# Low parts of the second weights on VectorE in two of three chunks, row sums pinned, stores behind the writes

## The chip, the cores and the metric

The kernel runs on one core of a Trainium2 chip. The metric is device time in microseconds, as the median of several executions. TensorE does the matmuls, VectorE (DVE) and GpSimd (POOL) the element-wise work on buffers in SBUF, ScalarE (ACT) activations and copies, and SyncE (SP) issues most of the DMA.

## What is computed

One encoder layer over 2304 rows (2048 of a prompt and 256 of a sample) of 1024 features, in float32. The mixing groups come first and are not touched by the change. Behind them stands the feed-forward part, then a final RMSNorm:

```python
x = x + group_output_norm(y_attn, y_four, y_mem, g_grp) @ w_out
hf = rmsnorm(x, g_ffn) @ w_ff1
x = x + jnp.square(jax.nn.relu(hf)) @ w_ff2
...
return rmsnorm(x, g_final)
```

## The kernel before

**The feed-forward part**, from about 865 us of the span to its end, handles the rows in NCH = 3 chunks (c = 0, 1, 2) of 768 rows: two halves of three blocks (NT = 3) of 128 rows. Both products are made by a scheme of Strassen's type: matrices are cut in 2 x 2 blocks, and seven products (i = 1 to 7) of sums of blocks replace eight. Each operand is a float32 number in two parts, a high part in TensorE's reduced format and the remainder as a low part, and each product is made of three matmuls: high by high, low by high, high by low. `hi_of` (L103) makes a high part on ACT, `lo_of` (L106) subtracts it from the source on VectorE, or on POOL if told so.

**The loop** (L1306 to L1340) goes over steps n. Step n makes one product of the first matmul (`product`, L1072: 12 matmuls of 128x384, into PSUM tiles pa, pb, pc, pd) and one half of a product of the second (`half_step`, L1167: 9 matmuls of 128x512, into y), 14 steps (LAG) behind. The halves of the last group of the last chunk run alone at the end, since no first products are left (`last_half_step`, which fills y and yl). Each half step needs one tile of the second weights w_ff2: `split2` (L1050) makes its high part w2h and low part w2l, each with two buffers; before the change w2l is made by POOL in all 336 half steps. `splitA` makes the high and low parts ah and al of the activations (POOL makes sums ms and m of them at L987). The loads of weights and of rows go through `granule` (L891) on SP's queue.

**The end of a chunk.** VectorE adds the products y into accumulators acc (L323, L326), and POOL and VectorE add accumulators to each other. `finish` (L1238) returns functions that the loop pops one for each step (`pending`, L1337): three calls of `write` (L1226) for each half of the rows. `measure` has ACT take sums of squares (tile fk, L1224), `write` has POOL make the reciprocal root (tile ff, L137 and L138), VectorE scale both halves of a row block (L1235), and then issues two stores to out_dram, that of the left half (n = 0) on ACT's queue and that of the right half on SP's. The next chunk's accumulators use the buffers of the ones written, and are loaded from X2d on SP's queue (`load_acc`).

**Row sums.** `late_rows` (L1283) is called three times in the middle of chunk 1, at n = 152, 160 and 168. Each call loads four tiles xl of the last chunk's normalized rows from XnT, lets POOL make four differences (`row_sums`, L819), and stores them to Xn, from where chunk 2 reads its operands XT.

**The order.** The program is written by a framework that runs a timeline estimate (`schedule_with_timeline_sim=True`, L1379) and sets each engine's order by it: an instruction that is ready early by that estimate can be moved ahead of where it is written. On the chip each engine then goes in that fixed order. Before the change, the first two groups of row sums stand in the change from chunk 0 to chunk 1, some 40 steps ahead of where they are written.

Of the kernel before, what the change touches and what calls it, by code (L numbers as in the profile page):

```python
# [20 lines left out]
P = 128  # L21
# [13 lines left out]
CH = 768  # L35
NCH = T // CH
CT = CH // P
NT = CT // 2
# [55 lines left out]
def trunk(ctx, tc, x, mem, w_in, w_mem, w_out, w1, w2, gains, g_final, sinks, ident_d, dist_d, cdft_d, seq_d, y):  # L94
    nc = tc.nc
    pe, act, dve, pool, sp = nc.tensor, nc.scalar, nc.vector, nc.gpsimd, nc.sync
# [5 lines left out]
    def hi_of(out, src, scale=1.0):  # L102
        act.activation(out, src, AF.Copy, scale=scale)  # L103

    def lo_of(out, src, hi, eng=None):
        (eng or dve).tensor_tensor(out=out, in0=src, in1=hi.bitcast(F32), op=ALU.subtract)  # L106
# [29 lines left out]
    def rstd_of_means(st):  # L136
        pool.tensor_scalar(out=st[:, 0:1], in0=st[:, 0:1], scalar1=st[:, 1:2], scalar2=EPS, op0=ALU.add, op1=ALU.add)  # L137
        pool.tensor_tensor(out=st[:, 0:1], in0=st[:, 0:1], in1=mhalf[:, 0:1], op=ALU.pow)  # L138
# [7 lines left out]
    if True:  # L146
# [100 lines left out]
        def stage(i, name):  # L247
            if i % 2:
                return stage4k(name)
            return apool.tile([P, D], F32, tag="Qs", bufs=2, name=name)  # L250
# [48 lines left out]
        for mp in (3, 2, 0, 1, 4):  # L299
            for kh in range(2):  # L300
                s = stage(kh, f"wins_{mp}_{kh}")
                sv = s.rearrange("p (k n) -> p k n", k=4)
                sp.dma_start(sv, w_in[kh * 512:(kh + 1) * 512, mp * 256:(mp + 1) * 256].rearrange("(k p) n -> p k n", p=P))
                for j in range(4):
                    k = kh * 4 + j
# [16 lines left out]
        def add(o, a, b):  # L322
            TT(out=o, in0=a, in1=b, op=ALU.add)  # L323
# [260 lines left out]
        for i, name in enumerate(order):  # L584
            g = int(name[1:])
# [17 lines left out]
    if True:  # L603
# [156 lines left out]
        def c_mem(pair, h, mh, ml):  # L760
            b0 = pair[0]["b"]
            vm = memkv[pair[0]["r"]][1]
            if h % 2 == 0:
                pair[0]["mo"] = ps_o.tile([P, 2, 256], F32, tag="o", name=f"otm_{b0}_{h}")
            po = pair[0]["mo"]
            for j in range(2):
                w = vm[:, j, h].rearrange("p l d -> p (l d)")
                mm(po[:, h % 2], w, mh[:, j], j == 0, False)
                mm(po[:, h % 2], w, ml[:, j], False, j == 1)
            if h % 2 == 1:  # L770
                pair[0].setdefault("ot", []).append(evac_o(po.rearrange("p a (b t) -> p (a b) t", b=2), f"otms_{b0}_{h}"))
            if h < 3:
                return None
            ots = pair[0]["ot"]

            def fin():
                for i, B in enumerate(pair):
                    ytile(B)
                    recip(B, NH, NMH)
                    combine(B, NH, [ots[g // 2][:, (g % 2) * 2 + i] for g in range(4)], f"om_{B['b']}")  # L780
                    normalise(B, 768, 256, 25)
            return fin
# [34 lines left out]
        def row_sums(b11, b21, b12, b22):  # L817
            for o, u, v, i in ((b11, b12, b11, 5), (b12, b22, b12, 7), (b22, b22, b11, 6), (b21, b22, b21, 4)):
                pool.tensor_tensor(out=o, in0=u, in1=v, op=ALU.subtract)  # L819
                yield i, o  # L820
# [70 lines left out]
        def granule(name, src, second=False):  # L891
            if second:
                t = rp.tile([P, 512], F32, tag="w2r", bufs=5, name=name)
            else:
                t = lp.tile([P, 512], F32, tag="w1r", bufs=9, name=name)
            if src is not None:
                sp.dma_start(t, src)
            return t
# [27 lines left out]
        n = 0  # L926
        while n < len(units) + LB or later:
            if n < len(units):
                kind, b0, i, h = units[n]
# [6 lines left out]
            if 0 <= m < len(units):  # L936
                kind, b0, i, h = units[m]
# [5 lines left out]
            if 0 <= m < len(units):  # L943
                kind, b0, i, h = units[m]
# [8 lines left out]
                if kind == "m":  # L953
                    f = c_mem(pairs[b0], h, *pend_b.pop(m))
# [17 lines left out]
    if True:  # L972
# [13 lines left out]
        def ptt(o, a, b, op):  # L986
            pool.tensor_tensor(out=o, in0=a, in1=b, op=op)  # L987
# [62 lines left out]
        def split2(r):  # L1050
            if 0 <= r < len(steps2):
                k = steps2[r]
                nm = "_".join(map(str, k))
                s = src2.pop(k)
                h = rp.tile([P, 512], F32R, tag="w2h", bufs=2, name=f"w2h_{nm}")
                l = rp.tile([P, 512], F32R, tag="w2l", bufs=2, name=f"w2l_{nm}")
                hi_of(h, s)
                lo_of(l, s, h, pool)
                ops2[k] = (h, l)


# [74 lines left out]
        acc, ybank = {}, {}  # L1136
# [19 lines left out]
        def last_group(c, g):  # L1156
            return c == NCH - 1 and g == NG - 1
# [57 lines left out]
        def gains_of(c):  # L1215
            return [granule(f"gf{n}_{c}", g_final[n * 512:(n + 1) * 512].partition_broadcast(P)) for n in range(2)]
# [3 lines left out]
        def measure(c, b, n, t):  # L1220
            if (c, b) not in stats:
                stats[c, b] = late[0].tile([P, 2], F32, tag="fst", bufs=6, name=f"ff_{c}_{b}")
            jk = late[0].tile([P, 512], BF16, tag="fjk", bufs=1, name=f"fk{n}_{c}_{b}")
            act.activation(jk, t, AF.Square, scale=D ** -0.5, accum_out=stats[c, b][:, n:n + 1])  # L1224

        def write(c, b, hv, gf, end=False):  # L1226
            r0 = c * CH + b * P
            st = stats.pop((c, b))
            rstd_of_means(st)
            for n in range(2):  # L1230
                o = hv[n]
                if end and n == 0:
                    act.activation(o, o, AF.Copy, scale=st[:, 0:1])
                else:
                    dve.scalar_tensor_tensor(out=o, in0=o, scalar=st[:, 0:1], in1=gf[n], op0=ALU.mult, op1=ALU.mult)  # L1235
                (sp if n else act).dma_start(y[r0:r0 + P, n * 512:(n + 1) * 512], o)

        def finish(c, g, i):  # L1238


            A = lambda i, t: acc[c, i, t]
            last = c == NCH - 1
            if i == 1 and g == NG - 1:
                acc[c, "g"] = gains_of(c)
            if last_group(c, g):
                for t in range(NT):
                    if i == 2:
                        measure(c, t, 0, A(2, t))
                        ptt(A(2, t), A(2, t), acc[c, "g"][0], ALU.mult)
                    elif i == 7:  # L1250
                        measure(c, NT + t, 1, A("x", t))
                    elif i == 4:
                        measure(c, NT + t, 0, A(4, t))
            else:
                for t in range(NT):
                    if i == 1:
                        acc[c, "x", t] = granule(f"x22_{c}_{t}", X2d[c * CT + NT + t][:, 512:1024])
                    elif i == 2:
                        ptt(A(2, t), A(2, t), A(1, t), ALU.add)
                    elif i == 5:  # L1260
                        ptt(A("x", t), A("x", t), A(5, t), ALU.add)
                    elif i == 6:
                        ptt(A(6, t), A(6, t), A(1, t), ALU.add)
                    elif i == 7:
                        add(A(7, t), A(7, t), A(6, t))
                        ptt(A(6, t), A(6, t), A(5, t), ALU.add)
                        add(A("x", t), A("x", t), A(7, t))
                    elif i == 4:
                        add(A(4, t), A(4, t), A(7, t))
                    elif i == 3:  # L1270
                        add(A(3, t), A(3, t), A(6, t))
                    if not last:
                        for o, h, k in ((2, 0, 2), (7, 1, "x"), (4, 1, 4), (3, 0, 3)):
                            if i == o:
                                measure(c, h * NT + t, 1 if k in ("x", 3) else 0, A(k, t))
            if g == NG - 1 and i == 4:
                return [lambda t=t: write(c, NT + t, [A(4, t), A("x", t)], acc[c, "g"]) for t in range(NT)]
            if g == NG - 1 and i == 3 and not last:
                return [lambda t=t: write(c, t, [A(2, t), A(3, t)], acc[c, "g"]) for t in range(NT)]
            return []  # L1280


        def late_rows(t):  # L1283
            a, b = (XnT[(NCH - 1) * CT + o + t].rearrange("p (n t) -> p n t", n=2) for o in (0, NT))
            g = [granule(f"xl{i}_{t}", s) for i, s in enumerate((a[:, 0], a[:, 1], b[:, 0], b[:, 1]))]
            for i, o in row_sums(*g):
                sp.dma_start(Xn[NCH - 1, i][:, :, t * P:(t + 1) * P], o.rearrange("p (k t) -> p k t", k=KH))

# [17 lines left out]
        for n in range(len(steps1) + LAG):  # L1306
# [17 lines left out]
            load_acc(r + 3)  # L1324
            operand1(n + 2)
            split2(r + 2)
            splitA(r + 2)
            sumA(r + 4)
            if n < len(steps1):
                product(n)  # L1330
                c, j, i = steps1[n]
                if j == NJ - 1 and c + 1 < NCH:
                    load_x(c + 1, i)
            if r >= 0:
                c, g, i, e = steps2[r]
# [48 lines left out]
```

## Time and profile before

| | |
|---|---|
| median of 3 runs | 2340.67 us (2337.38 to 2342.37) |
| the profiled execution | 2344.84 us |
| its span | 2343.0 us |
| TensorE busy | 2229.2 us, 95% |
| VectorE busy | 1561.4 us, 67% |
| POOL busy | 1139.7 us, 49% |
| ACT busy | 1003.4 us, 43% |

Durations are those of the profiled execution. Busy time of TensorE can hold slow matmuls: the granted clock, as a share of 2.4 GHz, tells how fast they ran. A row of a timeline gives the start in the span, the duration, the engine, the line, the operation, result and operands, the count, and in brackets the idle time before it and the instruction that ended it. Counts in brackets in a table of stretches are instructions.

### The profile page before, as it was taken

How to read it: one execution, taken by the hardware profiler on the slowest of the kernel's cores; microseconds unless marked ns; L12 is line 12 of the kernel's file. 1: busy time of each engine (PE TensorE's matmuls, PEld its weight loads, DVE VectorE, ACT ScalarE, POOL GpSimd, SP SyncE). 2: the span in 40 equal slices, each digit the busy share in tenths (PEclk: the TensorE clock that was granted, in tenths of full speed). 3: DMA queues.
4: the chain of work that ended last, by engine and by line, in shares of the span. 5: the costliest groups of instructions: out<-in, count | busy, mean ns of one | idle time of the engine just before them, and what ended most of it. 6: DMA issues, size and time to landing. Idle time of an engine off the chain costs nothing.

```text
span 2343.0 us, 35879 instructions
## 1 busy us (share of the span) xinstructions
PE 2229.2 (95%) x12464; PEld 2005.2 (86%) x12464; DVE 1561.4 (67%) x2781; ACT 1003.4 (43%) x2353; POOL 1139.7 (49%) x1023
## 2 busy tenths in 40 slices
PE   7999996999999999999999899999999999999996
PEld 6999995887788878999999788999998889999984
DVE  7333476777677767888888986555557765555567
ACT  6333356766566654444444433222224342222224
POOL 3554031113123035777777685444444765444476
PEclk9999998999999999999999999999999999999998
DMA  8886347445444368766666887555557675555543
GB/s 298 309 296 246 100 136 280 138 148 158 149 145 156 132 238 298 252 222 228 222 229 222 311 262 272 192 191 190 190 191 268 196 258 187 190 189 190 190 163 99
DMA packets 207116, 488.05 MB, mean 208 GB/s; under 512 B 19799, under 2 KB 63319, under 8 KB 204631
## 3 DMA queue, kind: packets, MB, share of 16 engines
q1 hardware_dynamic: 192896, 446.86, 56.2%
q0 software_dynamic: 6848, 29.24, 3.6%
q10 hardware_dynamic: 7191, 9.65, 1.2%
q8 instruction: 99, 1.62, 0.3%
q14 instruction: 82, 0.67, 0.1%
HBM read 341.76 MB, written 144.83 MB: 208 GB/s over the span
## 4 chain that ended last, share of the span: by engine, by line
PE 67%; DVE 8%; DMA 4%; ACT 2%; issue 2%; POOL 1%; SPq 0%; POOLq 0%; ACTq 0%; DVEq 0%
PE y L100 26%; PE op L100 8%; PE pc L100 8%; PE pb L100 8%; PE pa L100 8%; PE pd L100 4%; DMA X2d<-xr 1%; DVE acc L323 1%; PE s L100 1%; PE ot L100 1%; PE t L687 1%; DVE p L661 1%; DMA XTl<-Xn 1%; DVE al L106 1%; PE otm L100 1%
## 5 line engine op out<-in xcount | busy, mean ns | idle before, releaser
L106 POOL TENSOR_TENSOR w2l<-w,w2h 128x512 fp32r<-128x512 f32 x336 | 484.3, 1443 | 494.8 <-ACT w2h L103 490.2
L100 PE MATMUL y<-w2l,ah 128*128 128x512 f32 x966 | 380.9, 395 | 6.4 <-POOL w2l L106 6.4
L100 PE MATMUL y<-w2h,al 128*128 128x512 f32 x966 | 381.9, 396 | 0.0
L100 PE MATMUL y<-w2h,ah 128*128 128x512 f32 x966 | 360.7, 398 | 17.6 <-DVE acc L323 9.0
L103 ACT ACTIVATE ah<-m 128x384 fp32r<-128x384 f32 x240 | 125.8, 524 | 509.5 <-PE y L100 488.0
L106 DVE TENSOR_TENSOR al<-m,ah 128x384 fp32r<-128x384 f32 x240 | 182.9, 763 | 180.2 <-ACT ah L103 167.6
L323 DVE TENSOR_TENSOR acc<-acc,y 128x512 f32<-128x512 f32 x378 | 244.3, 680 | 24.1 <-PE y L100 20.0
L100 PEld LDWEIGHTS y<-w2h,ah 128*128 128x128 f32 x966 | 183.3, 190 | 45.2 <-DVE acc L323 12.1
L100 PE MATMUL pc<-XTh,w1s 128*128 128x384 f32 x768 | 218.8, 340 | 0.8 <-DVE m L323 0.3
L100 PE MATMUL pa<-XTh,w1s 128*128 128x384 f32 x768 | 215.7, 337 | 0.7 <-ACT w1s L103 0.5
L100 PE MATMUL pb<-XTh,w1s 128*128 128x384 f32 x768 | 214.5, 336 | 0.7 <-ACT m L1095 0.7
L103 ACT ACTIVATE w2h<-w 128x512 fp32r<-128x512 f32 x336 | 207.3, 617 | 10.9 <-DMA w1s<-W1D 4.5
L100 PEld LDWEIGHTS y<-w2h,al 128*128 128x128 f32 x966 | 183.3, 190 | 33.1
L100 PEld LDWEIGHTS y<-w2l,ah 128*128 128x128 f32 x966 | 183.3, 190 | 30.4 <-POOL w2l L106 7.8
L100 PE MATMUL pj<-hl_x,winh 128*128 128x256 f32 x720 | 206.1, 288 | 0.7 <-DVE hl_x L106 0.7
L100 PE MATMUL pj<-hh_x,winh 128*128 128x256 f32 x720 | 203.5, 288 | 1.3 <-ACT hh_x L103 1.3
L100 PE MATMUL pj<-hh_x,winl 128*128 128x256 f32 x720 | 204.5, 286 | 0.0
L1068 DVE SCALAR_TENSOR_TENSOR m<-m 128x384 f32<-128x384 f32 x192 | 159.0, 828 | 42.5 <-ACT m L1095 39.0
L100 PEld LDWEIGHTS pc<-XTh,w1s 128*128 128x128 f32 x768 | 142.9, 190 | 10.4 <-DVE m L323 1.4
L100 PEld LDWEIGHTS pb<-XTh,w1s 128*128 128x128 f32 x768 | 141.2, 188 | 8.9 <-ACT m L1095 1.0
L100 PEld LDWEIGHTS pa<-XTh,w1s 128*128 128x128 f32 x768 | 141.6, 188 | 8.3 <-ACT w1s L103 0.8
L100 PEld LDWEIGHTS pj<-hl_x,winh 128*128 128x128 f32 x720 | 139.3, 194 | 1.3 <-DVE hl_x L106 1.2
(243 smaller groups left out, 5181.4 us busy)
## 6 DMA issues: line engine op xcount, KB each, us to landing
w1s<-W1D SPq DMA_DIRECT2D x224, 512.0 KB, 3.5
W1D<-w1s SPq DMA_DIRECT2D x112, 512.0 KB, 3.6
w<-in_w_dram SPq DMA_DIRECT2D x208, 256.0 KB, 3.8
w<-W2T SPq DMA_DIRECT2D x192, 256.0 KB, 3.6
w2r<-in_w_dram SPq DMA_DIRECT2D x16, 1024.0 KB, 7.3
W2T<-w2r POOLq DMA_DIRECT2D x16, 1024.0 KB, 6.2
XTl<-Xn SPq DMA_DIRECT2D x21, 768.0 KB, 7.7
qb<-Qd SPq DMA_DIRECT2D x18, 768.0 KB, 6.3
```

Of the source, the lines that this page charges most:

```text
L100: pe.matmul(out, lhsT, rhs, start=start, stop=stop, skip_group_check=more)
L103: act.activation(out, src, AF.Copy, scale=scale)
L106: (eng or dve).tensor_tensor(out=out, in0=src, in1=hi.bitcast(F32), op=ALU.subtract)
L323: TT(out=o, in0=a, in1=b, op=ALU.add)
L661: dve.tensor_tensor_reduce(out=p[:, 0:n], in0=s[:, 0:n], in1=bias[:, u, c0:c0 + n], scale=1.0, scalar=nsink[:, u:u + 1], op0=ALU.add, op1= ...
L687: pe.transpose(t[:, j], p[:, j * P:(j + 1) * P], ident)
L1068: dve.scalar_tensor_tensor(out=r, in0=r, scalar=0.0, in1=r, op0=ALU.max, op1=ALU.mult)
```

## The change

It has three parts. The low part w2l is made by VectorE where the half step belongs to chunk 1 or 2 (k[0] is the chunk), 224 of 336; chunk 0's stay on POOL. The loads of `late_rows` are issued inside `tc.keep_in_program_order`, so that the scheduler leaves them where they are written. `finish` returns, through `rows`, first the three functions that write and then three that `store`: both halves of a row block go out by SP's queue, in functions popped three steps after the writes; only the very last rows (`end`) are stored by `write` as before.

```diff
--- before.py
+++ after.py
@@ -1055,7 +1055,7 @@
                 h = rp.tile([P, 512], F32R, tag="w2h", bufs=2, name=f"w2h_{nm}")
                 l = rp.tile([P, 512], F32R, tag="w2l", bufs=2, name=f"w2l_{nm}")
                 hi_of(h, s)
-                lo_of(l, s, h, pool)
+                lo_of(l, s, h, pool if k[0] == 0 else dve)
                 ops2[k] = (h, l)
 
 
@@ -1233,7 +1233,13 @@
                     act.activation(o, o, AF.Copy, scale=st[:, 0:1])
                 else:
                     dve.scalar_tensor_tensor(out=o, in0=o, scalar=st[:, 0:1], in1=gf[n], op0=ALU.mult, op1=ALU.mult)
-                (sp if n else act).dma_start(y[r0:r0 + P, n * 512:(n + 1) * 512], o)
+                if end:
+                    (sp if n else act).dma_start(y[r0:r0 + P, n * 512:(n + 1) * 512], o)
+
+        def store(c, b, hv):
+            r0 = c * CH + b * P
+            for n in range(2):
+                sp.dma_start(y[r0:r0 + P, n * 512:(n + 1) * 512], hv[n])
 
         def finish(c, g, i):
 
@@ -1274,15 +1280,22 @@
                             if i == o:
                                 measure(c, h * NT + t, 1 if k in ("x", 3) else 0, A(k, t))
             if g == NG - 1 and i == 4:
-                return [lambda t=t: write(c, NT + t, [A(4, t), A("x", t)], acc[c, "g"]) for t in range(NT)]
+                return rows(c, NT, 4, "x")
             if g == NG - 1 and i == 3 and not last:
-                return [lambda t=t: write(c, t, [A(2, t), A(3, t)], acc[c, "g"]) for t in range(NT)]
+                return rows(c, 0, 2, 3)
             return []
+
+        def rows(c, b0, i0, i1):
+            hv = [[acc[c, i0, t], acc[c, i1, t]] for t in range(NT)]
+            return ([lambda t=t: write(c, b0 + t, hv[t], acc[c, "g"]) for t in range(NT)] +
+                    [lambda t=t: store(c, b0 + t, hv[t]) for t in range(NT)])
 
 
         def late_rows(t):
             a, b = (XnT[(NCH - 1) * CT + o + t].rearrange("p (n t) -> p n t", n=2) for o in (0, NT))
-            g = [granule(f"xl{i}_{t}", s) for i, s in enumerate((a[:, 0], a[:, 1], b[:, 0], b[:, 1]))]
+            g = [granule(f"xl{i}_{t}", None) for i in range(4)]
+            for o, s in zip(g, (a[:, 0], a[:, 1], b[:, 0], b[:, 1])):
+                tc.keep_in_program_order(sp.dma_start(o, s))
             for i, o in row_sums(*g):
                 sp.dma_start(Xn[NCH - 1, i][:, :, t * P:(t + 1) * P], o.rearrange("p (k t) -> p k t", k=KH))
```

POOL's order in the change from chunk 0 to chunk 1, before (x and acc are accumulators, xl the row sums; a w is named by chunk, group, product and half, w2h and w2l leave the chunk out):

```order
L987 TENSOR_TENSOR acc_0_2_10703<-acc_0_2_10703,acc_0_2_10828 128x512
L106 TENSOR_TENSOR w2l_7_6_0_15233<-w_0_7_6_0_15137,w2h_7_6_0_15232 128x512
L819 TENSOR_TENSOR xl_1_17086<-xl_1_17090,xl_1_17086 128x512
L987 TENSOR_TENSOR x_0_0_15131<-x_0_0_15131,acc_0_0_10992 128x512
L106 TENSOR_TENSOR w2l_7_6_1_15272<-w_0_7_6_1_15177,w2h_7_6_1_15271 128x512
L987 TENSOR_TENSOR x_0_1_15133<-x_0_1_15133,acc_0_1_10997 128x512
L819 TENSOR_TENSOR xl_1_17090<-xl_1_17092,xl_1_17090 128x512
L987 TENSOR_TENSOR x_0_2_15135<-x_0_2_15135,acc_0_2_11002 128x512
L106 TENSOR_TENSOR w2l_7_7_0_15314<-w_0_7_7_0_15228,w2h_7_7_0_15313 128x512
L819 TENSOR_TENSOR xl_1_17092<-xl_1_17092,xl_1_17086 128x512
```

and now:

```order
L987 TENSOR_TENSOR acc_0_2_10703<-acc_0_2_10703,acc_0_2_10828 128x512
L106 TENSOR_TENSOR w2l_7_5_1_15182<-w_0_7_5_1_15085,w2h_7_5_1_15181 128x512
L106 TENSOR_TENSOR w2l_7_6_0_15233<-w_0_7_6_0_15137,w2h_7_6_0_15232 128x512
L987 TENSOR_TENSOR x_0_0_15131<-x_0_0_15131,acc_0_0_10992 128x512
L987 TENSOR_TENSOR x_0_1_15133<-x_0_1_15133,acc_0_1_10997 128x512
L106 TENSOR_TENSOR w2l_7_6_1_15272<-w_0_7_6_1_15177,w2h_7_6_1_15271 128x512
L987 TENSOR_TENSOR x_0_2_15135<-x_0_2_15135,acc_0_2_11002 128x512
L106 TENSOR_TENSOR w2l_7_7_0_15314<-w_0_7_7_0_15228,w2h_7_7_0_15313 128x512
L987 TENSOR_TENSOR acc_0_0_11082<-acc_0_0_11082,acc_0_0_10818 128x512
```

The subtractions of xl have gone from between the weights and the sums of accumulators; w2l of chunk 0 is still POOL's.

VectorE's order some steps later, at the first half steps of chunk 1, before:

```order
L106 TENSOR_TENSOR al_0_1_1_15633<-m_1_1_15454,ah_0_1_1_15632 128x384
L1235 SCALAR_TENSOR_TENSOR acc_0_0_11046<-acc_0_0_11046,ff_3_15472,gf_0_15127 128x512
L1235 SCALAR_TENSOR_TENSOR x_0_0_15131<-x_0_0_15131,ff_3_15472,gf_0_15129 128x512
L1235 SCALAR_TENSOR_TENSOR acc_0_1_11048<-acc_0_1_11048,ff_4_15478,gf_0_15127 128x512
L1235 SCALAR_TENSOR_TENSOR x_0_1_15133<-x_0_1_15133,ff_4_15478,gf_0_15129 128x512
L323 TENSOR_TENSOR acc_0_0_11147<-acc_0_0_11147,y_7_3_0_15600 128x512
L1235 SCALAR_TENSOR_TENSOR acc_0_2_11050<-acc_0_2_11050,ff_5_15484,gf_0_15127 128x512
```

and now (the w of each w2l names chunk 1):

```order
L1235 SCALAR_TENSOR_TENSOR acc_0_0_11046<-acc_0_0_11046,ff_3_15472,gf_0_15127 128x512
L1235 SCALAR_TENSOR_TENSOR x_0_0_15131<-x_0_0_15131,ff_3_15472,gf_0_15129 128x512
L106 TENSOR_TENSOR al_0_1_1_15631<-m_1_1_15454,ah_0_1_1_15630 128x384
L323 TENSOR_TENSOR acc_0_0_11147<-acc_0_0_11147,y_7_3_0_15600 128x512
L106 TENSOR_TENSOR w2l_0_1_0_15578<-w_1_0_1_0_15487,w2h_0_1_0_15577 128x512
L1235 SCALAR_TENSOR_TENSOR acc_0_1_11048<-acc_0_1_11048,ff_4_15478,gf_0_15127 128x512
L1235 SCALAR_TENSOR_TENSOR x_0_1_15133<-x_0_1_15133,ff_4_15478,gf_0_15129 128x512
L323 TENSOR_TENSOR acc_0_1_11149<-acc_0_1_11149,y_7_3_1_15604 128x512
```

The low part of the weights now stands in the row of scaled writes and additions to accumulators.

ACT's order at the same place, before:

```order
L103 ACTIVATE ah_0_1_1_15632<-m_1_1_15454 128x384
L103 ACTIVATE w2h_0_1_0_15577<-w_1_0_1_0_15487 128x512
L1236 DMA out_dram<-acc_0_0_11046 128x512
L103 ACTIVATE ah_0_2_0_15685<-m_1_0_15202 128x384
L103 ACTIVATE w2h_0_1_1_15628<-w_1_0_1_1_15525 128x512
L1236 DMA out_dram<-acc_0_1_11048 128x512
L1236 DMA out_dram<-acc_0_2_11050 128x512
L1095 ACTIVATE m_1_2_15801<-pa_2_15692 128x384
```

and now:

```order
L103 ACTIVATE ah_0_1_1_15630<-m_1_1_15454 128x384
L103 ACTIVATE w2h_0_1_0_15577<-w_1_0_1_0_15487 128x512
L103 ACTIVATE ah_0_2_0_15681<-m_1_0_15202 128x384
L103 ACTIVATE w2h_0_1_1_15626<-w_1_0_1_1_15525 128x512
L1095 ACTIVATE m_1_2_15791<-pa_2_15688 128x384
```

The issues of stores have left ACT's queue; they stand on SP's, each ahead of the load of an accumulator of the next chunk.

## Rows read from the trace of the kernel before

**Rows 1.** The page of the profile, busy time of each engine

```profile
PE 2229.2 (95%) x12464; PEld 2005.2 (86%) x12464; DVE 1561.4 (67%) x2781; ACT 1003.4 (43%) x2353; POOL 1139.7 (49%) x1023
```

**Rows 2.** Stretches; PE, PEld, DVE, ACT, POOL busy us (instructions); granted clock, DMA share, GB/s

```profile
1310.00:1340.00 30.00, 24.10 (x101) 19.71 (x100) 30.00 (x33) 12.81 (x22) 22.56 (x15) 0.89 0.85 323
1380.00:1430.00 50.00, 43.03 (x194) 36.67 (x194) 45.51 (x55) 19.72 (x45) 37.50 (x33) 0.93 0.83 270
1800.00:1810.00 10.00, 8.06 (x33) 6.95 (x32) 9.93 (x14) 4.73 (x8) 3.08 (x2) 0.83 0.78 274
1860.00:1890.00 30.00, 25.42 (x114) 21.71 (x113) 29.23 (x40) 14.75 (x35) 22.91 (x22) 0.89 0.63 209
2000.00:2050.00 50.00, 50.00 (x254) 45.50 (x253) 27.31 (x47) 14.14 (x27) 22.81 (x18) 1.00 0.57 190
2280.00:2330.00 50.00, 38.63 (x143) 27.89 (x143) 39.49 (x53) 20.38 (x46) 36.84 (x30) 0.93 0.21 58
```

**Rows 3.** TensorE's waits, 1000 to 2343 us: releaser, us, times, longest

```profile
PE y L100 <- DVE acc L323: 9.0, 7, 3.8
PE y L100 <- DVE acc L326: 7.6, 4, 3.3
PE y L100 <- POOL w2l L106: 6.4, 4, 2.9
PE yl L100 <- POOL w2l L106: 5.1, 5, 1.7
PE yl L100 <- DVE acc L323: 1.9, 1, 1.9
```

**Rows 4.** The timeline of TensorE: start, duration, instruction, idle before

```profile
1325.77 0.80 PE L100 MATMUL y<-w2h,ah 128*128 128x512 f32 x1 [3.82 <-DVE acc L323]
```

**Rows 5.** The timeline of VectorE and POOL, 1298 to 1307 us

```profile
1298.85 0.68 DVE L106 TENSOR_TENSOR w1s<-w1s,w1s 128x512 fp32r<-128x512 f32 x1
1299.45 0.55 DVE L106 TENSOR_TENSOR al<-m,ah 128x384 fp32r<-128x384 f32 x1
...
1305.32 1.29 POOL L106 TENSOR_TENSOR w2l<-w,w2h 128x512 fp32r<-128x512 f32 x1 [4.16 <-ACT w2h L103]
...
1305.35 1.68 DVE L106 TENSOR_TENSOR al<-m,ah 128x384 fp32r<-128x384 f32 x1
```

**Rows 6.** The timeline of POOL and VectorE at 1323 us

```profile
1322.72 1.58 POOL L819 TENSOR_TENSOR xl<-xl,xl 128x512 f32<-128x512 f32 x1
...
1323.10 2.01 DVE L106 TENSOR_TENSOR XTl<-XTl,XTh 128x768 fp32r<-128x768 f32 x1
```

**Rows 7.** VectorE's groups (busy us, mean ns), 2000 to 2050 us, then 2262 to 2330

```profile
L106 DVE TENSOR_TENSOR al<-m,ah 128x384 fp32r<-128x384 f32 x8 | 4.4, 554 | 8.9 <-ACT ah L103 8.9
...
L106 DVE TENSOR_TENSOR al<-m,ah 128x384 fp32r<-128x384 f32 x14 | 12.1, 873 | 4.4 <-ACT ah L103 4.4
L323 DVE TENSOR_TENSOR acc<-acc,acc 128x512 f32<-128x512 f32 x9 | 10.6, 1198 | 0.0
```

**Rows 8.** Stretches, w2l alone: POOL busy us (instructions), clock, DMA share, GB/s

```profile
1395.00:1430.00 35.00, 12.04 (x8) 1.00 0.89 293
1790.00:1825.00 35.00, 12.15 (x7) 0.95 0.80 290
1850.00:1890.00 40.00, 11.13 (x9) 0.91 0.67 221
2000.00:2050.00 50.00, 16.65 (x12) 1.00 0.57 190
2262.00:2330.00 68.00, 28.29 (x19) 0.95 0.25 78
```

**Rows 9.** The timeline of ACT and its queue of DMA issues

```profile
1398.95 3.44 ACTq L1236 DMA_DIRECT2D out_dram<-acc  x2
1402.43 0.49 ACT L1095 ACTIVATE m<-pa 128x384 f32<-128x384 f32 x1 [4.42 <-DVE acc L1235]
```

**Rows 10.** DMA issues: xcount, KB each, median us from issue to landing

```profile
out_dram<-acc ACTq DMA_DIRECT2D x18, 256.0 KB, 3.3
```

## The prediction

> **What bounds the kernel now.** I read the totals first: TensorE is busy for 95% of the span, VectorE for 67% [rows 1]. A shorter time needs stretches where TensorE stands still or runs slowly, so I looked for them in a table of stretches [rows 2]. From 2000 to 2050 us, the steady middle of a chunk, TensorE is busy for all of 50.00 us with 254 matmuls, 0.197 us each, while VectorE works for 27.31 us. In five other stretches it is not: around the change from chunk 0 to 1 (A, 1310 to 1340, and B, 1380 to 1430), from chunk 1 to 2 (C, 1800 to 1810, and D, 1860 to 1890), and in the last group (E, 2280 to 2330). At the steady rate A should have held 152 matmuls and held 101: 51 x 0.197 = 10 us lost. B lost 60 matmuls, 12 us; C 18, 3.5 us; D 38, 7.5 us. E has mostly the wide matmuls of the second product. A steady step is 12 matmuls of 384 columns and 9 of 512, 439 columns on average, so a wide one takes 0.197 x 512/439 = 0.23 us, and E's 143 take 33 us: 17 us lost. Together about **50 us** are open to the change; all other work of TensorE stays.
>
> The waits say what is late there: TensorE waits 30.0 us in all, 18.5 us for VectorE's additions to the accumulators and 11.5 us for POOL's w2l [rows 3]. The other 20 us follow the waits. After a stall of 3.82 us a matmul took 0.80 us [rows 4], and the granted clock of A is 0.89 of the full 2.4 GHz, of C 0.83 [rows 2]. So a microsecond of wait costs 50/30 = 1.65 us here.
>
> Why are the additions late? VectorE is busy for all of A (30.00 of 30) and nearly all of C and D. It isn't only loaded, it is held up by POOL. A subtraction of the same form as w2l's, 128x512 from two buffers in SBUF, took 0.68 us on VectorE while POOL stood still, the next started 0.60 us after it, and that one (al) took 0.55 us; beside POOL's w2l (1.29 us) another al took 1.68 us [rows 5]. That is 1.13 us more, about as long as the w2l beside it. Beside a row sum of 1.58 us a split of XT took 2.01 us [rows 6]. In the steady stretch al takes 554 ns, in the last group 873, and acc<-acc,acc 1198 [rows 7].
>
> **Part 1, w2l on VectorE in chunks 1 and 2.** It takes 224 instructions from POOL and gives them to VectorE at 0.60 us, the distance of starts in [rows 5]. In the steady stretch that is 12 x 0.60 = 7.2 us in 50 [rows 8]: VectorE goes from 27.31 to 34.5 us, 69%, and POOL from 22.81 to 6.2. TensorE still covers it, so the steady cost is nothing; without that cover it would be up to 0.60 us on each of some 180 steady instructions, 108 us, but 15 us free in each 50 speak against any of that.
> At the transitions VectorE has no such room. There are 8 of these w2l after B's start, 7 around C, 9 around D and 19 in the last group, 43 in all [rows 8]: 43 x 0.60 = 25.8 us more work. What it gives back is POOL's hold, between 0 (no VectorE instruction met) and 1.13 us each. In the last group al lost 14 x 0.32 = 4.5 us and acc<-acc,acc, against the 0.68 us of an undisturbed subtraction of that size, 9 x 0.52 = 4.7 us [rows 5, 7], some 0.5 for each of 19 w2l; I take 0.5 in E and D, where VectorE also has other delays, and 0.9 in B and C, near the upper row, as VectorE there runs from one instruction to the next. Net: (8 + 7) x 0.3 = 4.5 gained, (9 + 19) x 0.1 = 2.8 lost: **1.7 us gained** (bounds 25.8 lost to 22.8 gained).
> The VectorE Perf Modes page of the Trainium skill ("VectorE: DVE Perf Modes", section "The TRN2 errata — SBUF-src ops pay a fixed extra latency per instruction") charges an instruction that reads SBUF a fixed extra time; by its adjusted figures for two float32 operands I estimate 0.69 us at 512 elements. The trace's 0.68 us duration agrees, but its 0.60 us distance of starts is what a full engine pays; by 0.69 the 43 would cost 29.7 us and the sum below would come out 3.9 us slower, 2325.
> The second gain is the wait for w2l itself. ACT makes w2h, POOL then needs about 1.4 to 1.5 us for the low part (16.65 us for 12, 28.29 for 19 [rows 8]) behind its own queue of sums; VectorE needs 0.68 us. The waits on it are 11.5 us [rows 3], 19 us with the slow clock. VectorE's own queue takes their place in part, so I take two thirds: **12 us** (0 to 19).
>
> **Part 2, row sums pinned.** POOL's rows xl and the 12 loads and 12 stores on SP leave the transition from 0 to 1, as the first piece of order shows, and go to the steady middle of chunk 1, where POOL then has only 6 us of work in 50 and SP's queue has nobody behind it in need. There they cost nothing. In A and B each can give VectorE up to 2.01 - 0.9 = 1.1 us back (0.9 is an estimate: XT has 768 columns, 1.5 times the 512 that took 0.60 us). Not every sum meets an instruction that reads SBUF: half of 12 is **5.5 us** (0 to 13). In chunk 1's middle VectorE's loss is covered as above.
>
> **Part 3, stores behind.** Six stores leave ACT's queue at each transition. ACT stood still for 4.42 us there, as the issue of a store waited for VectorE's scaling of acc with the products' PSUM copies behind it [rows 9]. TensorE waits for ACT nowhere in [rows 3], so I take **1 us** (0 to 4.4 us). On SP the stores stand just ahead of loads of the next accumulators.
> The DMA page ("DMA: Bandwidth & Descriptors", section "Issuing engines are not separate DMA queues") of the Trainium skill says that another issuing engine saves just the time to issue. By that the part would be worth nothing, 1 us less in the sum; the 4.42 us in the row speaks against it, since the issue sat on ACT with its wait.
>
> **The sum.** 1.7 + 12 + 5.5 + 1 = 20 us. The profiled execution took 2344.84 us, 4.2 us over the median of 2340.67; so 2325 against it, and **2321 us** as a median. The start of the feed-forward part and the last writes are as before: 0. The part's own range, from half the wait gain and no row-sum gain (-8) to most of the open loss (-32), is 2309 to 2333. A change under 0.2%, 4.7 us, can't be told from none.
>
> **Rivals.**
> - Nearly all stalls go: the additions and w2l come on time, the clock stays at 1.00, and 38 of 50 us return: 2303 us. For it: both causes in [rows 3] trace back to POOL. Against: the 43 w2l add to a VectorE that is full in A, C, D.
> - One wait for another: w2l comes as late from VectorE as from POOL, as VectorE is busy 29.23 of 30 us in D [rows 2], and only A and B gain, by row sums, 4 us: 2337 us, no change. For it: 0.60 us is paid surely, the relief is worked out.
> - VectorE becomes the bound (slower). If POOL's hold isn't relieved where it counts, because the sums left on POOL hold VectorE just as long, the 43 w2l extend VectorE's chain by 25.8 us, less the 6.5 us of parts 2 and 3: 19 us, 2360 us. It decides from the point where VectorE in E (39.49 of 50) has no idle left; 19 x 0.6 = 11.4 us against 10.5 us idle is just there. Against: al ran at 0.55 us where POOL was idle.
> - The new SP queue: stores wait on SP for the scaling, loads of accumulators are behind them and need the buffers after 3.4 us of landing [rows 10]; three such in a row at two transitions are 20 us, which eats the gain: 2341 us, no change. Against: no DMA stands among TensorE's waits today.
>
> That the change does not do what it says is excluded by the order: POOL has 224 fewer instructions, VectorE 224 more.
>
> **How the numbers follow.** The forecast gets 0.60, nearly-all 0.14, one-for-another 0.11, the SP queue 0.06, VectorE bound 0.09. Faster by over 0.2%: 0.60 + 0.14 = 0.74; same 0.11 + 0.06 = 0.17; slower 0.09. The range must leave out 0.2: the VectorE case, the SP case and a part of the tails are out; 2302 to 2338 holds the forecast with its bounds, the nearly-all case and the one-for-another case.
>
> **What would show it.** Right: no xl on POOL before about 1450 us; VectorE's w2l at 0.68 us; al near 0.55 us in B and D; steady VectorE near 69% with TensorE at 50.00 of 50; waits on w2l under 4 us in all; ACT without idle on L1235's acc. Part 1 is wrong if VectorE is at 100% in E with waits on acc longer than before; part 2 if A still has 100% VectorE and 3 us stalls; part 3 if acc<-X2d shows up among TensorE's releasers. The whole is wrong if the steady stretch holds under 254 matmuls.

## The result and the profile after

The change takes **2325.21 us** (median of 4 runs, 2323.78 to 2328.20) against 2340.04 us (4 runs, 2337.38 to 2342.37) for the kernel before: a ratio of 0.9941, with a 95% interval of 0.9926 to 0.9956. That is 14.8 us faster, where 20 was forecast and 2321 us named; the time lies in the range. The profiled execution took 2326.01 us, its span is 2324.2 us.

TensorE's waits from 1000 us to the end, of the change (releaser, us in total, times, longest), answer to [rows 3]:

```profile
PE pc L100 <- DMA w1s<-W1D: 4.5, 2, 2.5
PE pc L100 <- DVE m L323: 4.4, 1, 4.4
PE yl L100 <- DVE w2l L106: 3.8, 4, 1.2
PE y L100 <- DVE acc L323: 3.3, 3, 1.3
PE yl L100 <- ACT w2h L103: 1.8, 3, 0.8
PE pb L100 <- DMA w1s<-W1D: 1.4, 1, 1.4
PE y L100 <- DVE w2l L106: 0.9, 2, 0.8
PE yl L100 <- DVE acc L323: 0.6, 2, 0.3
PE y L100 <- DVE acc L326: 0.4, 1, 0.4
PE pa L100 <- DMA w1s<-W1D: 0.4, 1, 0.4
```

The two causes of before have shrunk as forecast. Additions to accumulators were 18.5 us and are 3.3 + 0.6 + 0.4 = 4.3; w2l was 11.5 and is 3.8 + 0.9 = 4.7. But 14.2 + 6.8 = 21.0 us of waits gone should, at the prediction's price of 1.65 us for each microsecond of wait, have been worth 35 us. New waits stand in their place: 6.3 us for w1s, the first product's weights that SP loads, 4.4 us for m and 1.8 us for w2h. In all TensorE waits 21.5 us instead of 30.0; 8.5 x 1.65 = 14 us, near what the medians show.

The same stretches as in [rows 2], of the change (busy us and instructions of PE, PEld, DVE, ACT, POOL, then the granted clock, DMA share, GB/s); 2270 to 2320 holds the last group, some 15 us earlier than before:

```profile
1310.00:1340.00 30.00, 26.96 (x123) 24.60 (x124) 29.60 (x38) 11.55 (x20) 16.57 (x12) 0.89 0.74 257
1380.00:1430.00 50.00, 43.77 (x211) 37.72 (x212) 39.56 (x61) 20.73 (x46) 23.09 (x21) 1.00 0.79 264
1800.00:1810.00 10.00, 10.00 (x54) 9.26 (x53) 10.00 (x18) 4.12 (x7) 2.56 (x2) 1.00 0.72 248
1860.00:1890.00 30.00, 26.36 (x125) 23.48 (x124) 27.28 (x43) 9.50 (x21) 14.38 (x15) 0.94 0.90 304
2000.00:2050.00 50.00, 50.00 (x252) 45.29 (x252) 32.88 (x57) 14.91 (x30) 6.94 (x6) 1.00 0.57 190
2270.00:2320.00 50.00, 34.75 (x131) 24.15 (x129) 44.40 (x70) 23.25 (x52) 22.89 (x21) 0.92 0.32 100
```

The steady stretch reads as forecast: TensorE full, VectorE at 32.88 us of 50 (34.5 was worked out), POOL at 6.94. The clock at the change from chunk 1 to 2 is 1.00 (it was 0.83) and TensorE has 54 matmuls in 10 us instead of 33. From 1310 to 1340, VectorE is still busy for 29.60 of 30 us, and the last group's VectorE for 44.40 of 50.

**A ledger by stage.** One instruction runs in the same order in all the kernels here: ACT's w2h, 336 times, one for each half step. Its 85th, 197th and 309th start in steady stretches (each the first of the seventh group of its chunk), so the distances between them and to the end of the span divide the time into the first change of chunks (A and B), the second (C and D) and the end (E). These are the three starts in ACT's timeline of the change:

```profile
1254.10 0.62 ACT L103 ACTIVATE w2h<-w 128x512 fp32r<-128x512 f32 x1
...
1735.57 0.62 ACT L103 ACTIVATE w2h<-w 128x512 fp32r<-128x512 f32 x1
...
2208.13 0.62 ACT L103 ACTIVATE w2h<-w 128x512 fp32r<-128x512 f32 x1
```

| us | 85th | first change | second change | end | all three |
|---|---|---|---|---|---|
| before | 1257.3 | 487.3 | 478.2 | 120.3 | 1085.7 |
| the change | 1254.1 | 481.5 | 472.6 | 116.1 | 1070.1 |
| gain | | 5.8 | 5.6 | 4.2 | 15.6 |

There is one profile for each kernel. Kernels that hardly differ in a stage agree in it within some 1.1 us, while the time to the 85th w2h, which the change doesn't touch, scatters from 1250.5 to 1257.3 us over the profiles. So the stages tell apart what the medians leave open; a difference of a microsecond in a stage shows nothing.

### The profile page after: what moved, and what is told of

It is laid out like the page before. It is cut to its first block, busy times and chain, and to the rows that moved or that the text cites. A ratio compares the mean times of both kernels' runs of the same rounds, so it can differ in the third digit from the quotient of the medians.

```text
span 2324.2 us, 35672 instructions
## 1 busy us (share of the span) xinstructions
PE 2219.7 (96%) x12464; PEld 1998.6 (86%) x12464; DVE 1654.8 (71%) x3005; ACT 1002.0 (43%) x2353; POOL 851.0 (37%) x799
## 3 DMA queue, kind: packets, MB, share of 16 engines
q8 instruction: 98, 1.61, 0.3%
## 4 chain that ended last, share of the span: by engine, by line
PE 68%; DVE 8%; DMA 4%; issue 2%; ACT 2%; POOL 0%; SPq 0%; POOLq 0%; DVEq 0%; ACTq 0%
PE y L100 27%; PE pc L100 8%; PE pb L100 8%; PE pa L100 8%; PE op L100 8%; PE pd L100 4%; DMA X2d<-xr 2%; PE s L100 1%; DVE acc L323 1%; PE ot L100 1%; PE t L687 1%; DVE p L661 1%; DVE ptl L106 1%; PE otm L100 1%; DMA w1s<-W1D 1%
## 5 line engine op out<-in xcount | busy, mean ns | idle before, releaser
L100 PE MATMUL y<-w2h,ah 128*128 128x512 f32 x966 | 351.0, 393 | 3.9 <-DVE acc L323 3.3
L106 DVE TENSOR_TENSOR al<-m,ah 128x384 fp32r<-128x384 f32 x240 | 159.6, 665 | 175.7 <-ACT ah L103 160.6
L100 PE MATMUL pb<-XTh,w1s 128*128 128x384 f32 x768 | 220.3, 336 | 2.7 <-DMA w1s<-W1D 1.4
L987 POOL TENSOR_TENSOR ms<-m,m 128x384 f32<-128x384 f32 x48 | 58.4, 1217 | 435.4 <-DVE m L1068 378.1
L106 POOL TENSOR_TENSOR w2l<-w,w2h 128x512 fp32r<-128x512 f32 x112 | 169.0, 1512 | 111.3 <-ACT w2h L103 110.3
L106 DVE TENSOR_TENSOR w2l<-w,w2h 128x512 fp32r<-128x512 f32 x224 | 175.1, 782 | 0.0
L1068 DVE SCALAR_TENSOR_TENSOR m<-m 128x384 f32<-128x384 f32 x192 | 147.5, 769 | 19.4 <-ACT m L1095 17.1
```

Of the source, the lines that this page charges most:

```text
L100: pe.matmul(out, lhsT, rhs, start=start, stop=stop, skip_group_check=more)
L1068: dve.scalar_tensor_tensor(out=r, in0=r, scalar=0.0, in1=r, op0=ALU.max, op1=ALU.mult)
```

## The experiments

My theory A was that part 1 carries most of the gain by two routes (TensorE waits less for w2l, and POOL holds VectorE less), part 2 some by freeing VectorE, and, once I had the trace of the change, that part 3 costs something, because SP waits at its stores. All were timed beside the kernel before.

**Each part alone, and the change without part 3.** e1_low_parts takes from the diff its first hunk alone:

```diff
-                lo_of(l, s, h, pool)
+                lo_of(l, s, h, pool if k[0] == 0 else dve)
```

> Part 1 alone: w2l of chunks 1 and 2 on VectorE, row sums and stores as before. Theory A (this part carries most of the gain, since the waits on w2l shrink and POOL's hold on VectorE goes): 9 to 14 us under the kernel before, 2326 to 2331. Rival B (VectorE pays 0.60 us for each w2l at the transitions and gives the gain back; the gain seen comes from the row sums): within 4 us of before.

e2_row_sums has the hunk of `late_rows` alone, e3_stores that of `write`, `store` and `rows`:

> Part 2 alone: the loads of the row sums pinned to the middle of chunk 1. Theory A: 3 to 6 us under before, 2334 to 2337, all of it between 1300 and 1430 us of the span. Rival B (row sums held the additions back in A and B and carry the gain): 10 us or more under before. Rival C: nothing, as VectorE stays full there with POOL's w2l of chunk 0.

> Part 3 alone: writes first, stores of both halves on SP's queue. Theory A (SP's queue waits at a store for VectorE's scaling, and loads of w1s stand behind it): 3 to 8 us over before, with waits of TensorE on w1s<-W1D at both transitions. Rival B (the forecast: ACT is freed, SP has slack): 0 to 2 us under before, no such waits.

e4_parts_1_2 has the hunks of e1 and e2, and the stores of before:

> Parts 1 and 2 together, the stores as before: the change with part 3 undone. Theory A (stores on SP cost): 2315 to 2321, 4 to 10 us under the whole change, and no wait of TensorE on w1s<-W1D. Rival B (part 3 is worth nothing or a little): 2325 to 2328, as the whole change or slightly over it.

| | median us | ratio to before, 95% | first change | second | end |
|---|---|---|---|---|---|
| e1_low_parts | 2327.46 | 0.9946 (0.9934 to 0.9958) | 485.9 | 472.2 | 115.9 |
| e2_row_sums | 2332.18 | 0.9970 (0.9959 to 0.9981) | 478.4 | 477.5 | 120.4 |
| e3_stores | 2340.76 | 1.0007 (0.9999 to 1.0016) | 488.1 | 477.7 | 120.6 |
| e4_parts_1_2 | 2322.55 | 0.9933 (0.9921 to 0.9945) | 481.6 | 472.2 | 115.8 |

Three things follow. Part 3 is worth nothing: the change and e4 agree within 0.4 us in every stage, and e3 with the kernel before within 0.9, so both of my expectations for it fall, the cost of 3 to 8 us and the gain; e4 has 6.1 us of waits on w1s as well, so those are not part 3's doing. (By its median e4 stands between the two times put down for it.) Part 2 alone gains 8.9 us at the first change and nothing clear elsewhere; by the medians it is some 7 us, more than the 3 to 6 of theory A and less than the 10 of rival B. And **the parts don't add there**: part 1 alone, whose median lies where theory A had it, gains 1.4 us at the first change and part 2 alone 8.9, but both gain 5.7. On top of part 2, w2l on VectorE costs 481.6 - 478.4 = 3.2 us at the first change, and gains 5.3 at the second and 4.5 at the end.

**What of the row sums cost: POOL's work or the transfers?** e8_sums_pinned leaves 9 of the 12 loads in the change of chunks and moves the sums and their stores:

```diff
-            for i, o in row_sums(*g):
+            b11, b21, b12, b22 = g
+            for o, u, v, i in ((b11, b12, b11, 5), (b12, b22, b12, 7), (b22, b22, b11, 6), (b21, b22, b21, 4)):
+                tc.keep_in_program_order(pool.tensor_tensor(out=o, in0=u, in1=v, op=ALU.subtract))
```

> The kernel before with POOL's row sums and their stores pinned to chunk 1's middle, while 9 of the 12 loads stay in the change of chunks. Theory A (POOL's sums held VectorE): as part 2 alone, 2331 to 2334. Rival B (the 12 loads and their queue time on SP were the cost): 2337 to 2340.

2331.93 us, 0.9969 (0.9958 to 0.9981), the first change in 478.5 us: the same as part 2 alone. The early loads cost nothing. It was the sums on POOL with their stores; the run does not part those two.

**Where w2l belongs to VectorE.** On parts 1 and 2, e5_pool_in_c1_g0 keeps chunk 1's first group on POOL, e6_pool_in_g0 chunk 2's too, and e10_last_groups gives VectorE only the last two groups of the chunks:

```diff
-                lo_of(l, s, h, pool if k[0] == 0 else dve)
+                lo_of(l, s, h, pool if k[0] == 0 or k[:2] == (1, 0) else dve)
...
+                lo_of(l, s, h, pool if k[0] == 0 or k[1] == 0 else dve)
...
+                lo_of(l, s, h, dve if k[0] and k[1] >= 6 else pool)
```

> Parts 1 and 2, but w2l of chunk 1's first group (14 half steps, the stretch after the change from chunk 0 to 1) stays on POOL. Theory A (part 1 gives back in that stretch what part 2 gained: VectorE pays 0.60 us for each w2l where it has no idle time): 2316 to 2319, the stretch from chunk 0's last first-use of an accumulator to chunk 1's near 479 us, as with part 2 alone, instead of 486. Rival B (the two parts overlap because both free VectorE from POOL): as parts 1 and 2, 2321 to 2324, the stretch stays near 486 us.

> As the run before, and w2l of chunk 2's first group on POOL too. Theory A (VectorE is as full after the second change of chunks, so its w2l there cost as well): 2311 to 2316, the stretch to chunk 2's accumulators under 472 us. Rival B (there the low parts of VectorE gained, as POOL has sums and roots to do): 2 to 7 us over the run before, that stretch near 477 us.

> Parts 1 and 2 with w2l on VectorE in the last two groups of chunks 1 and 2 alone (56 of the 224), on POOL elsewhere. Theory A (the steady instructions moved give nothing, the gain of part 1 is at the end of chunk 1 and in the last group): 2318 to 2323, as the runs with POOL in the first groups; the stretch from chunk 2's accumulators to the end 415 us as in the whole change. Rival B (part 1 gains in the steady stretches also): 2326 or more, the stretch to the end 417 us or more.

The stretches that these expectations name run between first uses of accumulators, those of the table between starts of w2h, so their lengths can't be set side by side.

| | median us | ratio to before, 95% | first change | second | end |
|---|---|---|---|---|---|
| e5_pool_in_c1_g0 | 2320.61 | 0.9918 (0.9907 to 0.9930) | 479.1 | 472.7 | 115.8 |
| e6_pool_in_g0 | 2323.39 | 0.9926 (0.9914 to 0.9938) | 478.5 | 472.8 | 115.8 |
| e10_last_groups | 2324.53 | 0.9931 (0.9916 to 0.9945) | 479.6 | 472.7 | 115.7 |

With chunk 1's first 14 w2l back on POOL, the first change takes 479.1 us instead of 481.6: part 1 gives back there, as theory A said, though the size (2.5 us) and the medians (2 us, intervals that overlap) are less than the 4 us or more it put down. (The step itself stands in more than one pair: with these w2l on POOL, e5, e6, e10, e11 and e12 have 478.5 to 479.6 us at the first change, with them on VectorE the change, e4 and e9 481.5 to 482.0.) With chunk 2's first group on POOL no stage changes: theory A falls there, and so does rival B, though e6's median, 2.8 us over e5's, would have fitted B. And e10, where 56 of the 224 w2l move, has the stages of e6, where 196 do, within 1.1 us: **the steady instructions moved give nothing and cost nothing**, and so does chunk 2's first group. By the stages, all that part 1 gains comes from the last two groups of two chunks; e10's median stands between the two times put down for it. (The medians of e6 and e10 stand with the time to their 85th w2h, which is 1256.9 us in e10's profile and 1251.8 in e6's.)

**Who delays w1s?** In the change, at 1867.55 us, TensorE waits for a load of w1s. The timeline of VectorE, of SP's queue and of TensorE there, of the change:

```profile
1861.19 0.68 DVE L106 TENSOR_TENSOR w2l<-w,w2h 128x512 fp32r<-128x512 f32 x1
1861.79 0.74 DVE L1235 SCALAR_TENSOR_TENSOR acc<-acc,ff,gf 128x512 f32<-128x512 f32 x1
...
1860.36 0.34 SPq L1242 DMA_DIRECT2D out_dram<-x  x1
1861.89 0.33 SPq L897 DMA_DIRECT2D w<-W2T  x1
1862.33 0.37 SPq L1037 DMA_DIRECT2D w1s<-W1D  x1
...
1867.55 0.45 PE L100 MATMUL pc<-XTh,w1s 128*128 128x384 f32 x1 [2.52 <-DMA w1s<-W1D]
```

In these rows each load on SP's queue starts behind the one that stands before it. The load of w writes a buffer that VectorE's w2l (1861.19 plus 0.68 us) has to read first; it starts at 1861.89, and the load of w1s behind it at 1862.33. That took 5.2 us to land, at 1867.55, when TensorE's pc starts after 2.52 us of wait. The stores of part 3 stand in the same queue, ready just ahead. Two runs ask which of the two it is. e7_stores_pinned is the whole change with the stores kept where they are written (the first hunk here), e9_w_on_pool_queue the whole change with 28 loads of w on POOL's queue (the others):

```diff
-                sp.dma_start(y[r0:r0 + P, n * 512:(n + 1) * 512], hv[n])
+                tc.keep_in_program_order(sp.dma_start(y[r0:r0 + P, n * 512:(n + 1) * 512], hv[n]))
...
-                sp.dma_start(t, src)
+                (q or sp).dma_start(t, src)
...
-                src2[c, g, i, e] = granule(f"w2_{c}_{g}_{i}_{e}", s, True)
+                src2[c, g, i, e] = granule(f"w2_{c}_{g}_{i}_{e}", s, True, pool if c and g == 0 else None)
```

> The whole change, with the stores kept where they are written, so that they stand three steps behind the writes in SP's order and not ahead by the scheduler's estimate. Theory A (SP's queue waits at a store for VectorE's scaling and holds the loads of w1s): 2319 to 2322, no waits of SP at the store over 3 us, TensorE's 6 us of waits on w1s<-W1D gone. Rival B (w1s is late because SP waits for VectorE's w2l to free the buffers of w, part 1's doing): 2324 to 2327, the waits on w1s stay.

> The whole change, with the loads of w for the first groups of chunks 1 and 2 (28 loads) issued on POOL's queue instead of SP's. Theory A (at the changes of chunks SP waits at a load of w until VectorE's w2l has freed its buffer, and the loads of w1s behind it come late): TensorE's 6.3 us of waits on w1s<-W1D gone, 2317 to 2322. Rival B (what delays w1s is SP's wait at the stores, or VectorE's load alone costs the time): the waits on w1s stay at 4 us or more, 2324 to 2328.

| | median us | ratio to before, 95% | first change | second | end |
|---|---|---|---|---|---|
| e7_stores_pinned | 2332.32 | 0.9967 (0.9954 to 0.9980) | 483.6 | 473.0 | 119.8 |
| e9_w_on_pool_queue | 2319.35 | 0.9912 (0.9899 to 0.9925) | 482.0 | 469.1 | 115.7 |

e9 is 5.9 us under the whole change in the medians, and 3.5 us under it at the second change, where the wait on w1s is gone; one of 1.9 us is left at the first change, which got no faster, since TensorE waits 4.0 us for the additions there now. These are TensorE's waits from 1290 to 1450 us in e9 (same columns as above); in the change TensorE waits 2.7 us for the additions there and 3.8 for w1s:

```profile
PE pc L100 <- DVE m L323: 4.5, 1, 4.5
PE y L100 <- DVE acc L326: 2.3, 2, 1.2
PE pa L100 <- DMA w1s<-W1D: 1.9, 1, 1.9
PE y L100 <- DVE acc L323: 1.7, 1, 1.7
```

In e9 the scheduler also puts the loads of w1s sooner into SP's queue, once those of w are out of it. So at the second change the row of w behind w2l, and w1s behind w, was the cost. At the first change w1s is late too, but taking half of it away there gave the time to VectorE's additions. That the stores alone would do it falls with e5 and e6 as well: their SP waits at stores as long as e4's, 38.0 and 41.5 us against 35.1 (L1236, 1300 to 2330 us), while TensorE's wait on w1s falls from 6.1 us to 2.7 and 0.3, with the w2l that leave VectorE.

e7 was a miss for both theories: slower than the change by 7 us. The three longest waits of SP's queue from 1380 to 1440 us in it:

```profile
SPq L1154 <- DMA out_dram<-acc: 11.6, 4, 4.6
SPq L897 <- DVE w2l L106: 8.9, 5, 2.1
SPq L1037 <- PE pc L100: 5.3, 2, 3.2
```

Loads of the next accumulators (L1154) wait there 11.6 us for the stores of the old contents to land, with w1s behind them: 4.4 us of that wait stand in the change. This is the wait that the prediction's rival of the SP queue named. It is real, but of the 20 us that the rival put on it little reaches TensorE: its waits on w1s at the first change are 4.7 us instead of 3.8, and the stage is 2.1 us longer. In the change the scheduler had placed the stores sooner than three steps behind. At the end, the six stores of the last chunk, pinned behind the very last ones, go out from 2324.09 to 2328 us, just before the end at 2331.9: the 3.7 us that e7's last stage is longer.

**Putting it together.** e11_best is the whole change with chunk 1's first group on POOL as in e5 and chunk 2's first loads of w on POOL's queue as in e9; e12_best_old_stores is the same with the stores of before:

```diff
-                lo_of(l, s, h, pool if k[0] == 0 else dve)
+                lo_of(l, s, h, pool if k[0] == 0 or k[:2] == (1, 0) else dve)
...
+                src2[c, g, i, e] = granule(f"w2_{c}_{g}_{i}_{e}", s, True, pool if c == 2 and g == 0 else None)
```

> All three parts, with w2l of chunk 1's first group on POOL (as in e5_pool_in_c1_g0) and the loads of w for chunk 2's first group on POOL's queue (as in e9_w_on_pool_queue). Theory A (the two mend different stretches, so they add): 2313 to 2318; the stretch to chunk 1's accumulators near 480 us, that to chunk 2's near 469, that to the end 415. Rival B (they relieve the same queue on SP): 2318 to 2322.

> As e11_best, with the stores as in the kernel before (part 3 undone). If part 3 costs: 2 to 4 us under e11_best. If it is worth something, as forecast (1 us), or nothing: within 2 us of e11_best.

| | median us | ratio to before, 95% | first change | second | end |
|---|---|---|---|---|---|
| e11_best | 2318.38 | 0.9908 (0.9894 to 0.9921) | 479.0 | 468.7 | 115.7 |
| e12_best_old_stores | 2320.87 | 0.9920 (0.9906 to 0.9933) | 479.3 | 468.7 | 115.9 |

By stages the two mends add: 1063.4 us against the change's 1070.1, 6.7 less. The median, 2318.4, stands at the border between the two expectations (that of the two mends adding ended at 2318), and is 6.8 us under the change, the interval just clear of the change's; e9 can't be told from it. e11 and e12 agree in every stage within 0.3 us, the third time that the stores show nothing. Their medians differ by 2.5 us, which neither expectation for e12 has, and the other way than those of the change and e4 did (2.7); where the stages agree so closely, that is scatter of the part ahead.

## Why the prediction was right, and what in it was off

- **What bounds the kernel**: right. The loss stood at the changes of chunks and in the last group, in the two waits named, and that is where the 15.6 us came from; outside, the change did nothing.
- **Part 1, steady stretch at nothing**: right, by e10 against e6. The prediction called the whole wrong if the steady stretch held under 254 matmuls, and it holds 252. But the 14 half steps from the 281st w2h to the 295th take 58.32 us in the change and 58.28 us before, so the rate is the same and the count told of nothing.
- **Part 1, the sum of 13.7 us**: 12.2 by the median of e1, 11.7 by its stages. The wait for w2l fell by 6.8 of 11.5 us, 59%, where two thirds were taken. At the end TensorE's waits on the additions fell too, from 3.9 to 0.6 us (2210 to 2330 us), so both routes are in the rows; no run parts them.
- **The step that failed** is the net of 0.3 us gained for each w2l in B, the first steps of chunk 1. I took the relief from POOL's hold there at 0.9 us, near the largest single row, because VectorE was full. But 14 w2l on VectorE cost 2.5 to 3.2 us there (e4 against e5 and e2) where 8 x 0.3 = 2.4 us were booked as a gain, and e1, with the row sums still on POOL, gains 1.4 us. Both parts had been priced against the same trace of before, in which VectorE is busy for 45.51 of B's 50 us; in the change it is busy for 39.56 and no longer full. That there was less hold left to relieve fits this, but no run shows it by itself. What the runs show is TensorE's waits at the first change, 1290 to 1450 us, in e4 and then in e5:

```profile
PE pc L100 <- DVE m L323: 4.4, 1, 4.4
PE y L100 <- DVE acc L323: 2.3, 2, 1.3
PE pa L100 <- DMA w1s<-W1D: 2.1, 1, 2.1
PE pc L100 <- DMA w1s<-W1D: 1.8, 1, 1.8
PE y L100 <- DVE acc L326: 0.4, 1, 0.4
...
PE pc L100 <- DVE m L323: 4.2, 1, 4.2
PE y L100 <- POOL w2l L106: 2.9, 1, 2.9
PE y L100 <- DVE acc L323: 1.3, 1, 1.3
PE y L100 <- DVE acc L326: 0.4, 1, 0.4
```

  With w2l on VectorE, TensorE waits 3.9 us for w1s and 1.0 us more for the additions, instead of 2.9 us for POOL's w2l: 2.0 us more, near the 2.5 us of the stage. So the loss in B shows more in the queue of loads on SP, as at the second change, than in the 0.60 us that VectorE pays for each. But the additions are close behind: e9 halves the wait on w1s there and gains nothing. How the 2.5 us divide between the two stays open. At D the same w2l neither gain nor cost (e5 against e6).
- **What was late next** was named for SP's queue, but with the wrong head of the queue: the prediction had stores ahead of accumulators, the runs show w, waiting for w2l, ahead of w1s (3.5 us at the second change, e9). Part 1 moved the freeing of w's buffers to VectorE, and that I had not followed: "the waits on w2l" were costed for TensorE alone, not for SP.
- **The 4.4 us wait for m** at 1313 us stands on instructions that the change left on their engines, in an order that came out another way: two XTl and an al on VectorE stand beside two w2l of chunk 0 on POOL. Before, POOL made one w2l at that place and TensorE waited 0.15 us for m; in e2 it waits 2.1 us.

```profile
1308.10 2.88 DVE L106 TENSOR_TENSOR XTl<-XTl,XTh 128x768 fp32r<-128x768 f32 x2
...
1308.14 3.96 POOL L106 TENSOR_TENSOR w2l<-w,w2h 128x512 fp32r<-128x512 f32 x2 [0.52 <-ACT w2h L103]
...
1310.90 1.61 DVE L106 TENSOR_TENSOR al<-m,ah 128x384 fp32r<-128x384 f32 x1
...
1312.44 0.54 DVE L323 TENSOR_TENSOR m<-m,pc 128x384 f32<-128x384 f32 x1
1312.90 0.94 DVE L106 TENSOR_TENSOR XTl<-XTl,XTh 128x768 fp32r<-128x768 f32 x1
...
1313.04 0.69 PE L100 MATMUL pc<-XTh,w1s 128*128 128x384 f32 x1 [4.41 <-DVE m L323]
```

  al took 1.61 us and the two XTl 2.88 us, where the XTl at 1312.90 took 0.94 alone, and m stood behind them. By this, A still has a full VectorE (29.60 of 30 us) and a stall of over 3 us, which the prediction had named as the sign that part 2 is wrong; part 2 gains all the same, since the stalls on the additions are gone. Chunk 0's last group on VectorE was not tried.
- **Part 2, 5.5 us** within 0 to 13: 8.9 alone, 4.3 on top of part 1 (485.9 against 481.6). The 5.5 is a slip: half of 12 sums at 1.1 us are 6.6 us, and the whole sum 21 us. All twelve sums, and not only the first two groups, stood in the change of chunks before (1313 to 1390 us); in the change the first starts at 1497.7 us, as forecast.
- **Part 3, 1 us**: 0, within 0.9 us by three pairs. The idle of ACT on VectorE's scaling is no longer in ACT's waits of the change, but no one waited for ACT. The Trainium skill's rule ("DMA: Bandwidth & Descriptors", "Issuing engines are not separate DMA queues"), by which the part was worth nothing, agrees with these pairs. It does not cover e9, where 28 loads on another engine's queue gave 3.5 us at the second change, as they no longer stood ahead of the loads of w1s. The row of 4.42 us that I set against the rule was slack.
- **The price of one w2l**: between 1861.19 and the next start 0.60 us, as forecast. In duration it is undisturbed 0.68 us, on average 0.80 at the first change (5.59 us for 7), 0.68 at the second, 0.755 in the steady stretch and 0.74 in the last groups; the means hide that 200 of the 224 take 0.68 to 0.70 us, as forecast, and the other 24 from 1.04 to 1.78 us. Stretches of the change, VectorE's w2l alone (busy us and instructions, clock, DMA share, GB/s):

```profile
1380.00:1420.00 40.00, 5.59 (x7) 1.00 0.82 267
1850.00:1890.00 40.00, 5.45 (x8) 0.96 0.80 267
2000.00:2050.00 50.00, 9.06 (x12) 1.00 0.57 190
2250.00:2310.00 60.00, 13.29 (x18) 0.97 0.27 81
```

  The Trainium skill's 0.69 us ("VectorE: DVE Perf Modes", "The TRN2 errata — SBUF-src ops pay a fixed extra latency per instruction") is its figure for one instruction, and agrees with the undisturbed duration of 0.68. The errata-adjusted row of that section, 58 cycles and one for each of 512 elements at 0.96 GHz, gives an estimate of 0.59 us, which agrees with the 0.60 us between starts. No run here turns on the difference.
- **Two more signs** were missed in size: the waits on w2l are 4.7 us and not under 4, and al takes 717 ns in B (932 before) and not 550; in D it takes 549 ns (776 before).
- **The rivals**: slower did not come, nor did one wait for another in full; 60% of the waits gone were eaten by new ones (12.5 of 21.0 us), which is that rival in part.

## What to carry to other kernels

When two parts of a change act on the same stretch, price the second against the kernel that has the first, not against the trace of before. Moving work to another engine also moves the moment its inputs are free: follow the queue that waits for those buffers, and what is queued behind. And move such work only where it is waited for: a quarter of the moved instructions (56 of 224) gave the whole gain of part 1.

## What was not expected of the hardware

Taking away one wait of 2.5 us on a load at the second change gave 3.5 us (469.1 us in e9, 468.7 in e11 and e12): more than the wait itself, and near the 1.65 us for each microsecond that the prediction took. The twelve row sums, 1.27 to 1.74 us each, cost 8.9 us more where they stood beside VectorE's work than in the middle of chunk 1, and it made no difference that nine of their loads stayed (e8).
